# Block 1's attention rewritten: reversed queries, cumulative sums in two fp32r rounds, paired scores, first operands in halves

## The chip, the cores and the metric

One core of a Trainium2 chip runs the whole program in one launch. The metric is the device time of an execution in microseconds. A core has TensorE for matrix products, VectorE, ScalarE and GpSimd for the rest, SyncE for issuing loads, and 16 DMA engines that all queues share. Each engine works through its own list of instructions in order and waits at semaphores for others.

## The reference

Two transformer blocks over 256 tokens of width 1024, in fp32. Block 1: an RMS norm modulated by six vectors from `silu(c) @ w_ada`, one product with `w_in` for queries, keys and values of two attentions and two gates, and then the two attentions of 8 heads of 64. After them come gates, an output product, and a mixture of 64 experts. Block 2 is another norm, convolution, latent attention, a cross-attention to a memory `mem_2` (whose keys and values come from `w_mem_kv`), and 16 experts.

The change is in block 1's attentions and the opening. The first attention is stick-breaking, in blocks of 128 queries:

```
z = (q . k) * 0.125
log_rest = where(past, log_sigmoid(-z), 0)
log_skip = reversed cumulative sum of log_rest - log_rest
a = where(past, exp(log_sigmoid(z) + log_skip), 0);  o = a @ v
```

The second, of 256 tokens and so of a single block, is a softmax with a bias by distance:

```
s = (q . k) * 0.125 + rel_bias[head, t5_bucket(q_pos - k_pos)], -1e30 where k_pos > q_pos
o = softmax(s) @ v
```

## The kernel before

Activations lie with features on the partitions: x is `[128, 8, 256]`, eight chunks of 128 features by 256 tokens. Weights come in chunks of 1 MB (`[128, 2048]` fp32) through a ring of large tiles (`ring_tile`, `load`, L94 to L102), all issued by SyncE (`nc.sync`) in program order. A chunk is split in two halves into a high fp32r part (a cast on ScalarE, L210) and a low one (a subtraction on VectorE, L211), and every product is three rounds: high by high, high by low, low by high (`passes`, L217). A product whose operands are plain fp32 appears as two instructions in the trace, an fp32r one as one.

The opening: SyncE loads `vec`, `hm` (the memory, 1 MB), the first chunk of `w_mem_kv`, `x`, then pairs of `w_ada` chunks with the other `w_mem_kv` chunks between them. ScalarE's queue loads four small tables: `t5`, `w_router`, the router's bias row and `caprow`. `memk(i)` multiplies the memory by a chunk of `w_mem_kv` (48 products of 256 columns); it is called for 0, 1, 2, and after the loop for 2 and 3. `ada` (L304) multiplies a `w_ada` chunk by `silu(c)`, laid out with zeros in `scz`. When four pairs are done, `ada_cols` turns them into columns, and A1, `xr`, `h_hi` and `h_lo` follow (L383 to L388): h is the operand of all `w_in` products.

The bias of the second attention is a `[8, 384]` row table by distance, `rel`, made by one product of `t5` (L351) and stored to DRAM (L369). It is read back with overlapping rows as `relU` (row p begins p elements later) and turned upside down by four products with `flip`, a matrix with ones on the other diagonal (L379), copied by VectorE (L381).

`qkv` runs the chunks of one attention: `qk_chunk` (48 products a chunk, evacuated by ScalarE at L415) and `v_chunk`, with more `ada` between. In the first attention `scores` (L471) makes two groups of 64-row products, one for the heads on the lower 64 partitions and one for those on the upper, each in its own PSUM bank; the pool `s` has three banks. `softplus` computes log(1+exp(z)) with three ScalarE steps, one VectorE step and a mask on GpSimd; products with `ntri` (a triangle of -1) and `nones` (all -1) add the cumulative sum to the scores in PSUM (L518, L524, L525); `stick` takes the exponential and masks; `av` multiplies by the values. Block 128..255 goes first (`z1`), then the first 128 keys in two halves of heads (`z0`). The second attention (`mb_p`) adds the bias, does a softmax over the free axis, transposes the probabilities with `ident` (L559, L560, L567) and calls `av`.

The order on each engine is made when the program is built, from its dependencies and modelled times: later `w_in` chunks stand between the steps of an attention. `order(late, early)` fixes the order of two instructions by hand, `tc.issue_after` issues what is in its body behind a given instruction. Tiles made by `big(slot, ...)` share a slot; a new tile in it waits until the old one is read.

After block 1 the router's choice sets the order in which the experts' weights are loaded, and the expert loops follow.

## Time and profile before

| | us |
|---|---|
| median of 3 runs | 1609.36 (1609.12 to 1611.26) |
| profiled execution | 1608.48 |
| its span, first to last instruction | 1606.6 |
| TensorE busy | 1403.8 |
| VectorE busy | 595.0 |
| ScalarE busy | 415.0 |
| DMA | 524.78 MB, mean 327 GB/s |

The profile shows one execution. Busy times are unions of an engine's instructions; TensorE's instructions overlap, so the pace of products is read from their starts and not from their durations. "Idle before" is the time for which an engine stood before an instruction, with the one that ended it. The chain of waits begins at 801.22 us.

### The profile page before, as it was taken

How to read it: one execution, taken by the hardware profiler on the slowest of the kernel's cores; microseconds unless marked ns; L12 is line 12 of the kernel's file. 1: busy time of each engine (PE TensorE's matmuls, PEld its weight loads, DVE VectorE, ACT ScalarE, POOL GpSimd, SP SyncE). 2: the span in 40 equal slices, each digit the busy share in tenths (PEclk: the TensorE clock that was granted, in tenths of full speed). 3: DMA queues.
4: the chain of work that ended last, by engine and by line, in shares of the span. 5: the costliest groups of instructions: out<-in, count | busy, mean ns of one | idle time of the engine just before them, and what ended most of it. 6: DMA issues, size and time to landing. Idle time of an engine off the chain costs nothing.

```text
span 1606.6 us, 24192 instructions
## 1 busy us (share of the span) xinstructions
PE 1403.8 (87%) x9933; PEld 886.7 (55%) x9933; DVE 595.0 (37%) x1093; ACT 415.0 (26%) x741; POOL 98.7 (6%) x157
## 2 busy tenths in 40 slices
PE   6999999898999989999899999999796776676674
PEld 4787899653554435455498899998441221121221
DVE  6433655522222223343565666674330110110122
ACT  4453444321111112122255344453200000000001
POOL 1000101200000000000011110111100000000001
PEclk9999999999999999999999999999897787778776
DMA  8885755389999999999943345656499999999995
GB/s 326 345 344 207 292 192 199 109 357 419 419 419 420 419 420 419 421 420 420 410 171 134 129 171 192 217 217 254 182 420 421 422 420 420 421 422 420 420 421 215
DMA packets 74162, 524.78 MB, mean 327 GB/s; under 512 B 8282, under 2 KB 9890, under 8 KB 10562
## 3 DMA queue, kind: packets, MB, share of 16 engines
q1 hardware_dynamic: 72848, 519.35, 80.5%
q10 hardware_dynamic: 1202, 3.87, 0.6%
q8 instruction: 79, 1.29, 0.3%
q14 instruction: 33, 0.27, 0.0%
HBM read 521.01 MB, written 2.17 MB: 326 GB/s over the span
## 4 chain that ended last, share of the span: by engine, by line
DMA 25%; PE 21%; DVE 2%; issue 2%; ACT 1%; POOL 0%; DVEq 0%; SPq 0%; ACTq 0%; POOLq 0%
DMA w<-in_w_gu 15%; PE ps_d L217 13%; DMA w<-in_w_down 10%; PE ps_u L1613 1%; PE ps_s L217 1%; PE ps_s L1392 1%; PE ps_s L1391 1%; PE ps_t L1399 0%; ACT whl L210 0%; PE ps_t L1382 0%; PE ps_y L1682 0%; PE ps_s L1516 0%; PE ps_c L1604 0%; POOL tsm L1374 0%; DVE whl L211 0%
## 5 line engine op out<-in xcount | busy, mean ns | idle before, releaser
L211 DVE TENSOR_TENSOR whl<-w,whl 128x1024 fp32r<-128x1024 f32 x156 | 193.8, 1246 | 146.9 <-ACT whl L210 146.5
L950 PE MATMUL ps_u<-w,xg 128*32 128x512 f32 (+1 forms) x1152 | 213.1, 627 | 22.3 <-DMA w<-in_w_gu 22.3
L217 PE MATMUL ps_d<-h_hi,whl 128*128 128x256 f32 x1216 | 225.5, 284 | 1.1 <-ACT whl L210 1.1
L210 ACT CAST whl<-w 128x1024 fp32r<-128x1024 f32 x156 | 162.7, 1048 | 169.9 <-PE ps_d L217 149.5
L217 PEld LDWEIGHTS ps_d<-h_hi,whl 128*128 128x128 f32 x1216 | 189.2, 189 | 6.8 <-ACT whl L210 2.8
L217 PE MATMUL ps_d<-h_lo,whl 128*128 128x256 f32 x608 | 171.7, 282 | 0.0
L950 PEld LDWEIGHTS ps_u<-w,xg 128*32 128x32 f32 (+1 forms) x1152 | 62.9, 126 | 167.3 <-issue 122.8
L1613 PE MATMUL ps_u<-w,xgb 128*32 128x512 f32 x512 | 96.5, 832 | 50.8 <-DMA w<-in_w_gu 50.8
L217 PEld LDWEIGHTS ps_d<-h_lo,whl 128*128 128x128 f32 x608 | 114.3, 188 | 1.5 <-issue 1.3
L1613 PE MATMUL ps_u<-w,xga 128*32 128x512 f32 x512 | 94.4, 697 | 21.1 <-DMA w<-in_w_gu 21.1
L1682 PE MATMUL ps_y<-w,aT 128*32 128x256 f32 x1024 | 84.6, 473 | 27.0 <-DMA w<-in_w_down 22.9
L973 PE MATMUL ps_y<-w,aT 128*32 128x512 f32 (+1 forms) x576 | 95.9, 597 | 0.7 <-DMA w<-in_w_down_e 0.7
L956 DVE SCALAR_TENSOR_TENSOR act<-ps_u,wsl,sl 128x256 f32<-128x256 f32 x26 | 12.6, 484 | 200.5 <-ACT sl L954 200.5
L1670 DVE SCALAR_TENSOR_TENSOR act<-ps_u,wsl,sl 128x256 f32<-128x256 f32 x16 | 7.7, 484 | 212.6 <-ACT sl L1660 212.6
L1613 PEld LDWEIGHTS ps_u<-w,xgb 128*32 128x32 f32 x512 | 12.6, 125 | 124.7 <-DMA w<-in_w_gu 119.2
L1660 ACT ACTIVATE sl<-ps_u 128x256 f32<-128x256 f32 x16 | 6.1, 383 | 276.0 <-PE ps_u L1613 276.0
L991 DVE TENSOR_TENSOR y<-ps_c,y 128x512 f32<-128x512 f32 x92 | 63.0, 686 | 32.3 <-PE ps_c L982 32.3
L1682 PEld LDWEIGHTS ps_y<-w,aT 128*32 128x32 f32 x1024 | 33.9, 131 | 73.7 <-DMA w<-in_w_down 42.6
L954 ACT ACTIVATE sl<-ps_u 128x256 f32<-128x256 f32 x26 | 10.0, 384 | 215.6 <-PE ps_u L950 215.6
L981 PE MATMUL ps_c<-S,yy 128*128 128x256 f32 x208 | 62.7, 325 | 1.1 <-ACT whl L210 0.6
L211 DVE TENSOR_TENSOR yy<-ps_y,yy 128x512 fp32r<-128x512 f32 x52 | 36.0, 692 | 51.6 <-ACT yy L210 51.6
L884 PE MATMUL ps_g<-G,ht_hi 128*128 128x256 f32 x208 | 51.9, 283 | 3.2 <-DVE G L865 2.9
(492 smaller groups left out, 2227.5 us busy)
## 6 DMA issues: line engine op xcount, KB each, us to landing
w<-in_w_gu SPq DMA_DIRECT2D x256, 1024.0 KB, 19.8
w<-in_w_down_e SPq DMA_DIRECT2D x64, 1024.0 KB, 19.8
w<-in_w_down SPq DMA_DIRECT2D x64, 1024.0 KB, 19.8
w<-in_w_in SPq DMA_DIRECT2D x42, 1024.0 KB, 6.2
w<-in_w_ada SPq DMA_DIRECT2D x24, 1024.0 KB, 9.7
w<-in_w_mem_kv SPq DMA_DIRECT2D x4, 1024.0 KB, 14.1
w<-in_w_out SPq DMA_DIRECT2D x4, 1024.0 KB, 7.7
w<-in_w_conv_out SPq DMA_DIRECT2D x4, 1024.0 KB, 4.8
```

Of the source, the lines that this page charges most:

```text
L210: nc.scalar.copy(hi, src)
L211: eng.tensor_sub(lo, src, hi.bitcast(F32))
L217: nc.tensor.matmul(region, l, r, start=(start and u == 0), stop=(stop and u == 2), skip_group_check=True)
L884: nc.tensor.matmul(ps[:, a, :ng], ht_hi[:, b, k * P:(k + 1) * P], m, start=(b == 0), stop=False)
L950: nc.tensor.matmul(pg[o:o + w], xg[:, 4 * half + k, o:o + w], ws[j][:, k], start=(half == 0 and k == 0), stop=(half == 1 and k == 3), tile ...
L973: nc.tensor.matmul(py[o:o + w], self.aT[:, f, o:o + w], wd[j][:, f, h * 512:(h + 1) * 512], start=(f == 0), stop=(f == 1), tile_position=( ...
L981: nc.tensor.matmul(ps[:, a], self.yy[:, 0, k * P:(k + 1) * P], self.S, start=True, stop=False)
L991: nc.vector.tensor_add(y1[:, 2 * q:2 * q + 2], ps, y1[:, 2 * q:2 * q + 2])
L1391: nc.tensor.matmul(ps[:, b], qnT[:, h, b * P:(b + 1) * P], knT[:, h], start=True, stop=False)
L1392: nc.tensor.matmul(ps[:, b], qrT[r, h // 2, b * P:(b + 1) * P], krT[r, 0], start=False, stop=True)
L1613: mm = nc.tensor.matmul(pg[32 * j:32 * j + 32], xg[k][:, 32 * e:32 * e + 32], w[:, 512 * j:512 * j + 512], start=(k == 0), stop=(k == KD - ...
L1682: nc.tensor.matmul(py[32 * j:32 * j + 32, :256], aT[:, f, 32 * v:32 * v + 32], w[:, f, 256 * j:256 * j + 256], start=(v == 0 and f == 0), ...
```

## The change

`hm` and the first `w_mem_kv` chunk are each loaded by two DMAs of half the size, and that chunk's two halves are split ahead of the squares of `hm`. Three fp32 products of `ones` with `scz` (504 columns), whose result nobody reads, stand ahead of the first real products. The four small tables on ScalarE's queue are issued behind the last `hm_hi` instruction. `rel` is stored two rounds later; `relU` and the four flip products with their copies are gone. The bias is read straight into its tile, behind the first `qkv`, with its rows upside down; to match, the queries of the second attention are written in reversed order inside each block of 128 (a negative step on L415's output), and the transposes of the probabilities use `flip` in place of `ident`, which turns them back. In `softplus` the result is split into a high and a low fp32r part, and `ntri` and `nones` are fp32r, with two products each. All products of a `scores` call are ordered one behind another, lower and upper 64 rows in turn.

```diff
@@ -318,21 +318,31 @@
...
     hm = big(2, [P, KD, T], F32, "hm")
-    nc.sync.dma_start(hm, I["memT"])
+    for u in range(2):
+        nc.sync.dma_start(hm[:, 4 * u:4 * u + 4], I["memT"][:, 4 * u:4 * u + 4])
     hm_hi, hm_lo = big(4, [P, KD, T], F32R, "hm_hi"), big(11, [P, KD, T], F32R, "hm_lo")
-    wk = [load(I["w_mem_kv"][0])]
+    wk = [ring_tile()]
+    for u in range(2):
+        o = slice(1024 * u, 1024 * u + 1024)
+        nc.sync.dma_start(wk[0][:, o], I["w_mem_kv"][0][:, o])
     nc.sync.dma_start(xT, I["xT"])
...
                 lambda j, ps: nc.vector.tensor_mul(mem_k[:, 2 * i:2 * i + 2], ps,
-                                                   rm[:, None, :].to_broadcast([P, 2, T])), loaded=wk[i])
-
+                                                   rm[:, None, :].to_broadcast([P, 2, T])), loaded=wk[i],
+                parts=wk0 if i == 0 else None)
+
+
+    ps = bank("t")
+    for _ in range(3):
+        nc.tensor.matmul(ps[:, :504], ones, scz.rearrange("p k n -> p (k n)"), start=True, stop=True)
     gm = col("norm_memkv_g", KD)
     for k in range(KD):
-        nc.scalar.activation(hm_hi[:, k], hm[:, k], AF.Copy, scale=gm[:, k:k + 1])
+        hm_last = nc.scalar.activation(hm_hi[:, k], hm[:, k], AF.Copy, scale=gm[:, k:k + 1])
         nc.vector.scalar_tensor_tensor(hm_lo[:, k], hm[:, k], gm[:, k:k + 1], hm_hi.bitcast(F32)[:, k],
                                        op0=ALU.mult, op1=ALU.subtract)
+    wk0 = SP.chunk(wk[0], KD, 256)
     acc = pa.tile([P, T], F32, name="acc", tag="acc", bufs=2)
@@ -346,13 +356,13 @@
...
     t5 = big(9, [32, 776], F32, "t5")
-    nc.scalar.dma_start(t5, I["t5"])
+    with tc.issue_after(hm_last.ins):
+        nc.scalar.dma_start(t5, I["t5"])
     ps_r = bank("t")
...
     rel_d = dram.tile([8, 384], F32, name="rel_d")
-    relU = big(3, [P, 8, 256], F32, "relU")
     memk(0)
@@ -365,20 +375,11 @@
...
                 memk(i + 1)
-        if i == 0:
+        if i == 2:
             nc.sync.dma_start(rel_d, rel)
-        if i == 2:
-            nc.sync.dma_start(relU, bass.AP(tensor=rel_d.tensor, offset=rel_d.offset,
-                                            ap=[[1, P], [384, 8], [1, 256]]))
     ada_cols(ps_a, 0, 4)
...
     memk(3)
-    bias = big(11, [P, 8, 256], F32, "bias")
-    for i in range(4):
-        ps = bank("t")
-        f = nc.tensor.matmul(ps, flip, relU[:, 2 * i:2 * i + 2].rearrange("p a n -> p (a n)"), start=True, stop=True)
-        order(f, mm)
-        nc.vector.tensor_copy(bias[:, 2 * i:2 * i + 2].rearrange("p a n -> p (a n)"), ps)
     A1 = pa.tile([P, KD], F32, name="A1")
@@ -396,11 +397,12 @@
...
     wr = pa.tile([P, KD, 64], F32, name="wr")
-    nc.scalar.dma_start(wr, I["w_router"])
     rbias = const.tile([P, 64], F32, name="rbias")
-    nc.scalar.dma_start(rbias, I["router_bias"].to_broadcast([P, 64]))
     caprow = const.tile([1, 64], F32, name="caprow")
-    nc.scalar.dma_start(caprow, I["caprow"])
+    with tc.issue_after(hm_last.ins):
+        nc.scalar.dma_start(wr, I["w_router"])
+        nc.scalar.dma_start(rbias, I["router_bias"].to_broadcast([P, 64]))
+        nc.scalar.dma_start(caprow, I["caprow"])
@@ -412,7 +414,11 @@
...
         def evac(j, ps):
-            nc.scalar.activation(qk[nm][:, 2 * c:2 * c + 2], ps, AF.Copy, scale=0.125 if nm[0] == "q" else 1.0)
+            o = qk[nm][:, 2 * c:2 * c + 2]
+            if nm == "q_mb":
+                o = bass.AP(tensor=o.tensor, offset=o.offset + P - 1, ap=[o.ap[0], [P, 4], [-1, P]])
+                ps = ps.rearrange("p a (b t) -> p (a b) t", b=2)
+            nc.scalar.activation(o, ps, AF.Copy, scale=0.125 if nm[0] == "q" else 1.0)
         SP.feat(I["w_in"][base + c], h_hi, h_lo, 256, KD, evac)
@@ -450,39 +456,43 @@
...
-    ntri = pa.tile([P, P], F32, name="ntri")
-    nc.gpsimd.memset(ntri, -1.0)
-    nc.gpsimd.affine_select(out=ntri, in_=ntri, pattern=[[-1, P]], base=0, channel_multiplier=1,
+    nones = pa.tile([P, P], F32R, name="nones")
+    nc.vector.tensor_scalar(nones, ones, -1.0, 0.0, op0=ALU.mult, op1=ALU.add)
+    ntri = pa.tile([P, P], F32R, name="ntri")
+    nc.gpsimd.affine_select(out=ntri, in_=nones.bitcast(F32), pattern=[[-1, P]], base=0, channel_multiplier=1,
                             compare_op=ALU.is_ge, fill=0.0)
-    nones = pa.tile([P, P], F32, name="nones")
-    nc.vector.memset(nones, -1.0)
-    o_hi = big(5, [P, 8, T], F32R, "o_hi")
-    o_lo = big(6, [P, 8, T], F32R, "o_lo")
-    spl, aTs, keep = quarters(12, "spl"), quarters(13, "aTs"), None
-
-    oc = {"sb": (o_hi[:, :4], o_lo[:, :4]), "mb": (o_hi[:, 4:], o_lo[:, 4:])}
+    aTs, keep = quarters(13, "aTs"), None
...
         pss = [bank("s").rearrange("p (h q) -> p h q", q=nr) for _ in range(2)]
+        mms = []
         for i in range(n):
...
                 q = slice(64 * r, 64 * r + 64)
-                nc.tensor.matmul(pss[r][:, i], lhs[q, i0 + i, l0:l0 + nl], rhs[q, i0 + i, r0:r0 + nr],
-                                 start=(i == 0), stop=(stop and i == n - 1))
+                mms.append(nc.tensor.matmul(pss[r][:, i], lhs[q, i0 + i, l0:l0 + nl], rhs[q, i0 + i, r0:r0 + nr],
+                                            start=(i == 0), stop=(stop and i == n - 1)))
+                if len(mms) > 1:
+                    order(mms[-1], mms[-2])
         return pss
-    def softplus(ps, nq, name):
+    sp_hi, sp_lo = big(12, [P, 4, 512], F32R, "sp_hi"), big(7, [P, 4, 512], F32R, "sp_lo")
+
+    def softplus(ps, nq, q):
+
         t = pa.tile([P, 512], F32, name="sp_t", tag="t512", bufs=3)
...
         nc.scalar.activation(t, t, AF.Ln, bias=1.0)
-        sp = (keep() if nq == P else spl()).rearrange("p (h q) -> p h q", q=nq)
-        nc.vector.scalar_tensor_tensor(sp.rearrange("p h q -> p (h q)"), f, 0.0, t, op0=ALU.max, op1=ALU.add)
-        nc.gpsimd.affine_select(out=sp, in_=sp, pattern=[[0, 512 // nq], [1, nq]], base=0, channel_multiplier=-1,
+        nc.vector.scalar_tensor_tensor(t, f, 0.0, t, op0=ALU.max, op1=ALU.add)
+        t = t.rearrange("p (h q) -> p h q", q=nq)
+        nc.gpsimd.affine_select(out=t, in_=t, pattern=[[0, 512 // nq], [1, nq]], base=0, channel_multiplier=-1,
                                 compare_op=ALU.is_gt, fill=0.0)
-        return sp
+        hi = sp_hi[:, q].rearrange("p (h q) -> p h q", q=nq)
+        lo = sp_lo[:, q].rearrange("p (h q) -> p h q", q=nq)
+        split(t, hi, lo)
+        return hi, lo
@@ -509,21 +519,29 @@
...
     qkv("sb", v_sb, 0)
+    bias = big(11, [P, 8, 256], F32, "bias")
+    nc.sync.dma_start(bias, bass.AP(tensor=rel_d.tensor, offset=rel_d.offset, ap=[[1, P], [384, 8], [1, 256]]))
+    o_hi = big(5, [P, 8, T], F32R, "o_hi")
+    o_lo = big(6, [P, 8, T], F32R, "o_lo")
+    oc = {"sb": (o_hi[:, :4], o_lo[:, :4]), "mb": (o_hi[:, 4:], o_lo[:, 4:])}
     mem_kd = dram.tile([P, KD, T], F32, name="mem_kd")
...
     z1 = scores(qk["k_sb"], qk["q_sb"], 4, 0, P, P, P, P)
-    s1 = [softplus(z1[r], P, "sp1") for r in range(2)]
+    s1 = [softplus(z1[r], P, r) for r in range(2)]
     for r in range(2):
-        nc.tensor.matmul(flat(z1[r]), ntri, flat(s1[r]), start=False, stop=True, skip_group_check=True)
+        for u in range(2):
+            nc.tensor.matmul(flat(z1[r]), ntri, flat(s1[r][u]), start=False, stop=(u == 1), skip_group_check=True)
     a1 = [stick(z1[r], P) for r in range(2)]
...
         z0 = scores(qk["k_sb"], qk["q_sb"], 2, 2 * j, 0, P, 0, T)
-        s0 = [softplus(z0[r], T, "sp0") for r in range(2)]
+        s0 = [softplus(z0[r], T, 2 + r) for r in range(2)]
         for r in range(2):
-            nc.tensor.matmul(flat(z0[r]), ntri, flat(s0[r]), start=False, stop=False, skip_group_check=True)
-            nc.tensor.matmul(z0[r][:, :, P:], nones, s1[r][:, 2 * j:2 * j + 2], start=False, stop=True,
-                             skip_group_check=True)
+            for u in range(2):
+                nc.tensor.matmul(flat(z0[r]), ntri, flat(s0[r][u]), start=False, stop=False, skip_group_check=True)
+            for u in range(2):
+                nc.tensor.matmul(z0[r][:, :, P:], nones, s1[r][u][:, 2 * j:2 * j + 2], start=False, stop=(u == 1),
+                                 skip_group_check=True)
         a0 = [stick(z0[r], T) for r in range(2)]
@@ -548,6 +566,7 @@
...
+    spl = quarters(12, "spl")
     qkv("mb", v_mb, 6)
@@ -556,15 +575,15 @@
...
             for i in range(2):
-                nc.tensor.transpose(ps[:, i, :P], p0[r][:, 2 * j + i], ident)
-                nc.tensor.transpose(ps[:, i, P:], p1[r][:, i, :P], ident)
+                nc.tensor.transpose(ps[:, i, :P], p0[r][:, 2 * j + i], flip)
+                nc.tensor.transpose(ps[:, i, P:], p1[r][:, i, :P], flip)
             a = aTs().rearrange("p (h q) -> p h q", h=2)
...
             for i in range(2):
-                nc.tensor.transpose(ps[:, 2 * r + i], p1[r][:, i, P:], ident)
+                nc.tensor.transpose(ps[:, 2 * r + i], p1[r][:, i, P:], flip)
         a1 = aTs().rearrange("p (h q) -> p h q", h=4)
...
         av("mb", v_mb, j, a0, [a1[:, 2 * r:2 * r + 2] for r in range(2)])
```

## Rows read from the trace of the kernel before

**Rows 1.** The page's first part: busy us (share of the span) and instructions.

```profile
PE 1403.8 (87%) x9933; PEld 886.7 (55%) x9933; DVE 595.0 (37%) x1093; ACT 415.0 (26%) x741; POOL 98.7 (6%) x157
```

**Rows 2.** Busy time by stage: length, busy (instructions), granted clock, DMA share, GB/s.

```profile
15.08:65.24 50.16, 48.15 (x340) 36.92 (x341) 29.24 (x58) 19.93 (x40) 0.74 (x2) 1.00 0.92 372
...
107.75:131.00 23.25, 23.00 (x136) 15.56 (x133) 9.53 (x11) 16.20 (x29) 7.31 (x12) 1.00 0.64 258
131.00:167.50 36.50, 36.50 (x307) 30.20 (x307) 13.15 (x12) 14.99 (x18) 0.00 (x0) 1.00 0.77 282
167.50:191.50 24.00, 22.44 (x173) 17.79 (x170) 18.53 (x36) 11.54 (x38) 6.53 (x16) 1.00 0.59 220
...
282.00:310.00 28.00, 21.90 (x124) 18.51 (x121) 17.42 (x88) 13.13 (x28) 11.38 (x17) 0.88 0.37 137
...
350.00:800.00 450.00, 423.53 (x2670) 213.56 (x2662) 142.22 (x313) 77.21 (x148) 0.00 (x0) 0.97 1.01 420
```

**Rows 3.** Timeline of the opening: start, us, engine, line, names, count [idle before].

```profile
4.13 0.17 DVE L298 COPY scz<-sc 128x8 f32<-128x8 f32 x1 [2.24 <-ACT sc L295]
...
7.03 3.30 ACT L333 ACTIVATE hm_hi<-hm,c_vec 128x256 fp32r<-128x256 f32 x8 [2.93 <-DMA hm<-in_memT]
...
14.09 1.05 ACT L210 CAST whl<-w 128x1024 fp32r<-128x1024 f32 x1
...
16.21 2.51 DVE L211 TENSOR_TENSOR whl<-w,whl 128x1024 fp32r<-128x1024 f32 x2
...
28.50 0.39 PE L217 MATMUL ps_d<-hm_hi,whl 128*128 128x256 f32 x1
```

**Rows 4.** Busy time in stretches of 2 us of the opening, as in rows 2.

```profile
18.00:20.00 2.00, 2.00 (x11) 2.00 (x10) 1.93 (x7) 2.00 (x7) 0.00 (x0) 1.00 1.02 430
...
22.00:24.00 2.00, 2.00 (x14) 1.35 (x14) 1.61 (x4) 0.58 (x2) 0.00 (x0) 1.00 0.00 0
24.00:26.00 2.00, 2.00 (x20) 2.00 (x19) 0.00 (x0) 0.63 (x1) 0.00 (x0) 1.00 0.61 125
```

**Rows 5.** SyncE's waits from 0 to 60 us: total, times, longest.

```profile
SPq L369 <- DVE acc L150: 16.1, 1, 16.1
```

**Rows 6.** DMA issues at 7.1, at 37.7 and at the end: KB each, us to landing.

```profile
w<-in_w_mem_kv SPq DMA_DIRECT2D x1, 1024.0 KB, 14.1
...
w<-in_w_ada SPq DMA_DIRECT2D x1, 1024.0 KB, 13.0
...
out<-of SPq DMA_DIRECT2D x4, 256.0 KB, 2.6
```

**Rows 7.** Timeline around the first w_in product, columns as in rows 3.

```profile
54.30 1.07 PE L304 MATMUL ps_a<-w,scz 128*32 128x512 f32 x8
...
59.25 3.92 PE L379 MATMUL ps_t<-relU,flip 128*128 128x512 f32 x8
63.11 1.04 PE L304 MATMUL ps_a<-w,scz 128*32 128x512 f32 x2
...
64.15 2.94 ACT L210 CAST whl<-w 128x1024 fp32r<-128x1024 f32 x3
...
65.24 0.39 PE L217 MATMUL ps_d<-h_hi,whl 128*128 128x256 f32 x1 [1.08 <-ACT whl L210]
```

**Rows 8.** Attention products: groups by form (busy us, mean ns | idle), then single lines.

```profile
L524 PE MATMUL ps_s<-spl,ntri 128*128 128x512 f32 x8 | 4.4, 631 | 0.0
L471 PE MATMUL ps_s<-qk_sb 64*128 64x256 f32 x16 | 4.2, 396 | 0.0
...
L471 PE MATMUL ps_s<-qk_sb 64*128 64x128 f32 x16 | 1.2, 285 | 0.0
...
L471 PE MATMUL ps_s<-qk_mb 64*128 64x256 f32 x16 | 3.8, 396 | 0.0
...
L471 PE MATMUL ps_s<-qk_sb x4: 376/377/378, 108.7 to 109.4; 64*128 64x256 f32 x4
...
L471 PE MATMUL ps_s<-qk_sb x2: 376/428/480, 115.0 to 115.3; 64*128 64x256 f32 x2
```

## The prediction

> **What bounds the kernel now.** I read the page's head first: TensorE is busy 87% of the span [rows 1]. The chain of waits reaches back only to the second half of the run and says nothing of the part that changes. So busy time by stage comes next [rows 2]. TensorE is busy 48.2 of 50.2 us in the opening, 23.0 of 23.25 in the first attention, 36.5 of 36.5 in the second set of projections and 22.4 of 24.0 in the second attention. Block 1 up to its routing is thus bound by TensorE's own instructions, apart from the first 15 us, in which it has none. From 282 to 310 us (routing) the DMA share is 0.37, and from 350 to 800 us it is 1.01 at 420 GB/s. The expert weights' stream is the bound there and does not push from behind: a microsecond cut from block 1 should move the routing, the stream and all that follows by a microsecond. Last I read the timeline of the opening and the groups by form of the two attentions.
>
> **The opening.** The first products wait in turn for three things. hm lands at 7.03 us; ScalarE then makes hm_hi until 10.3, squares and loads a table, so that the first half of the first weights is cast only at 14.09 and its low part begins on VectorE at 16.21 [rows 3]. TensorE is then slow: 11 products start in 18 to 20 us, 20 in 24 to 26 [rows 4]. Both rows print a granted clock of 1.00, but about 0.213 us a start is the pace of 256 columns at the 1.2 GHz level, and the 0.117 of later that of the 2.4 GHz one; the engine had been idle for 15 us. Meanwhile SyncE stands 16.1 us before it stores rel, and every load behind it on that queue stands too [rows 5]; the DMA share is 0.00 in 22 to 24 us [rows 4].
>
> After the change hm lands without 0.39 MB of small tables beside it, about 1 us earlier (0.39 MB at 420 GB/s), and its first half some 1.2 us before that. hm_hi then ends near 8.1 us, two casts of 1.05 near 10.2, the first low part (1.25) near 10.4: the first products start at about 10.5. The idle products can start when scz is written, at 4.3 us [rows 3]. They are six instructions of 0.85 us (twice the 0.43 derived below, at the lower level), so they end near 9.5 and delay nothing. The first 48 products then end near 16.2 us. I cost the four table issues on ScalarE's queue at nothing: ahead of the casts they would delay a first round that has until 20 us.
>
> For that gain is not kept whole. The second weights of this kind were issued at 7.02 us and took 14.1, landing at 21.1 [rows 6], behind the same 7 MB as after the change. I take 20 us, between 18.4 (all at full rate) and 21.1. Cast and low part add some 2, so the second round starts at about 21.8 instead of 28.50 [rows 3]: 6.7 us won. The first ada and the statistics, some 4 us of products, fit into the gap.
>
> From 28.5 to 59.25 us TensorE has 30.75 us of products almost without a wait. Then come 3.92 us of bias products, an ada load's 1.04 and 1.08 idle, while h is made; from the last ada product of this stretch (54.30 plus 1.07) to the first w_in product (65.24) it is 9.9 us, ended by ScalarE [rows 7]. Removing the bias products, and four VectorE copies beside them, shortens that chain by nothing: they are its cover. They pay only if the last ada products move ahead of other work. These can: their load, issued at 37.7 us, took 13.0 and landed at 50.7 [rows 6]. Without the stall and without relU's 1 MB, eight 1 MB loads at 2.5 us follow the one that I put at 20 us: it lands at 40. What TensorE then has left is 21.8+30.75+2.1 (two ada loads) = 54.6 us, 10.6 less than 65.24. If it keeps its order, the gain stays 6.7. I take 9.5, nearer to the end that the loads allow.
>
> relU's transfer now fetches bias behind the first qkv's loads; the DMA share is 0.77 in the next projections [rows 2], which hide it, and its reader is 60 us away. Uncovered it costs 2.5 us. The store of rel, two rounds later, is behind some 8 MB already issued, 20 us of transfers; a stall like the old one of 16.1 fits into that: 0.
>
> **Attention.** One fp32 round becomes two fp32r rounds. Four fp32 instructions of 256 columns start within 0.65 us, 0.216 apart, so 512 columns take 0.43 [rows 8]. ntri has 12 of 512 (8 of them in the row; two instructions for each of six products), nones 8 of 256 by its four calls: 5.2+1.7 = 6.9 us. In fp32r a 256-column start takes 0.117, so the same count costs 12*0.234+8*0.117 = 3.7, and 3.2 us are won. Scores: the 128-column ones already run in pairs, 16 in 1.2 us; the 256-column ones do not, 16 in 4.2 and 16 in 3.8 us [rows 8]. Fully paired they would take 2.4 each: 3.2 us. But a group needs two of three banks, and its first product may still go alone as soon as one is free, three steps for four: 1.6. I take 2.4, between them.
>
> The splits add six ScalarE copies, half of the 1.05 us cast each, 3.2 us in all, and six VectorE subtractions, and each softplus is later by about 1.3 us. ScalarE is busy 16.2 of 23.25 us there [rows 2], 19.4 after it. A late product on TensorE holds up what stands behind it, the casts likewise behind the copies; 12 half-chunks of the next weights (2.8 us of products for each cast) are there to fill. I charge 1.5 us of new idle, between 0 and the 5.6 won. The reversed write of the queries is not in the trace: two copies on a ScalarE with 21.5 of 36.5 us free [rows 2], 0 if as fast as now, 3.2 us if four times slower (half a cast, twice), and hidden; I take 0. Flip for ident in the transposes leaves count and shape: 0. keep no longer holds the softplus, so this no longer waits for mem_k's store: 0.
>
> **Sum.** 9.5+3.2+2.4-1.5 = 13.6 us. The profiled execution took 1608.48 us, 1.9 more than its span, and is 0.88 under the median of the runs shown: 1608.5-13.6+0.9 = 1595.8 us.
>
> **Rivals.**
> (a) The split softplus makes ScalarE the bound: the 5.6 us of the first attention and the scores come back as waits. For it: ScalarE's 16.2 us. Against: the filler. 1608.5-9.5+0.9 = 1599.9 us.
> (b) TensorE keeps its order around the last ada and stands idle where the bias products were: 2.8 us less, 1598.6.
> (c) The halves load worse than whole tiles. A 256 KB store lands 2.6 us after its issue [rows 6], 0.6 of it data; if 2 us were added for each of two extra pieces, all loads come 4 us later: 1599.8. Against: the loads behind one another come at 430 GB/s [rows 4], so a fixed part is hidden in the queue. The Trainium skill's page DMA: Bandwidth & Descriptors, section Bandwidth, speaks against this edit: pieces of at least 1 MiB keep three quarters of the peak. No run here shows a load of half that size.
> (d) The idle products end too long before the real ones, and the engine is slow again: 48 products at 0.213 us end at 20.7, an ada round of 1.9 at 22.6, and the second round starts 0.8 us later: 1596.6. The Trainium skill's page TensorE: Matmul & The Clock Gate, section Why this matters for your kernels, warns that idle gaps between bursts take the rate back. The slow products after 15 us of idling [rows 4] agree with it.
> (e) Slower: the fixed order makes the first half of a 256-column group wait for the second's bank. In the old trace one half went at 108.7 us and the other at 115.0 [rows 8]. Four groups held back 6.3 us each cost 25 us with nothing to fill them, 1621; under 14 of filler in these 25 the gain is gone. Against: the filler of 131 to 167.5 us is 36.5 us long [rows 2].
> (f) No change: waits in the routing take the gain back, 1609.
>
> **Numbers.** Forecast 0.53, (a) 0.12, (b) 0.12, (c) 0.06, (d) 0.07, (e) 0.05, (f) 0.05. The forecast's own range is 1591 to 1600: its best end is 10.6 with the second weights at 18.4 (1.6 more) and 6.4 in the attentions, 1590.8. The 1.6 us that TensorE idles in the second attention may go too: 1589. (a) and (b) or (c) together reach 1604. Range 1588 to 1604, without (e) and (f). 0.2%, 3.2 us, is about what a measurement tells from no change: faster 0.88, same 0.06, slower 0.06.
>
> **What will show it.** The first real product near 10.5 us, 0.117 us from start to start; the second round near 21.8; no DMA share under a half from 12 to 40 us; the first w_in product near 55.7 (58.5 by b). In the attention, fp32r products of 512 columns 0.23 us apart, 256-column scores in pairs, under 2 us idle on TensorE. The routing as long as before, 13 to 14 us earlier. I am wrong if the first w_in product comes under 5 us earlier, if the attentions add over 6 us of idle, or if the full stream that runs from 350 us starts no earlier.

## The result and the profile after

The changed kernel takes 1618.35 us, median of five runs (1617.38 to 1619.07), against 1610.2 of the kernel before: ratio 1.0051, 95% interval 1.0039 to 1.0062. It is 0.5% slower. The forecast was 1595.8, at most 1604.

TensorE has as much to do as before [rows 1]. Engines of the changed kernel: busy us (share), instructions.

```profile
PE 1404.5 (87%) x9931; PEld 890.1 (55%) x9931; DVE 599.0 (37%) x1095; ACT 418.3 (26%) x747; POOL 100.7 (6%) x156
```

The changed kernel by stage, in the order of [rows 2]: opening, first attention, second projections, second attention, routing, stream.

```profile
12.67:70.69 58.02, 50.77 (x333) 39.34 (x333) 30.57 (x61) 23.56 (x48) 6.65 (x8) 0.85 0.82 331
114.85:143.30 28.45, 24.09 (x155) 18.73 (x152) 15.60 (x18) 22.22 (x36) 6.72 (x10) 0.88 0.61 245
143.30:179.60 36.30, 36.06 (x288) 27.76 (x286) 12.45 (x12) 13.73 (x18) 1.75 (x2) 1.00 0.75 281
179.60:203.60 24.00, 21.79 (x173) 17.03 (x170) 18.70 (x36) 11.42 (x38) 6.53 (x16) 1.00 0.60 228
294.00:322.00 28.00, 22.05 (x123) 18.66 (x122) 17.35 (x88) 13.16 (x28) 11.36 (x17) 0.88 0.36 133
360.00:810.00 450.00, 422.39 (x2686) 213.78 (x2678) 141.22 (x310) 77.76 (x149) 0.00 (x0) 0.98 1.01 418
```

Two stages are longer, the opening (58.0 us for 50.2) and the first attention (28.5 for 23.3). In both TensorE now idles, 7.3 and 4.4 us (2.0 and 0.3 before), and the mean granted clock printed fell from 1.00 to 0.85 and 0.88. The opening's 1.00 before is too high: it also stands over the slow products up to 22 us, 22 starts in 18 to 22 us where 0.117 us a start gives 34. Starts of the same instructions in the two traces say where the 10.7 us between the spans come from:

```
first instruction of      before    after   shift
first memory chunk         15.95    12.67    -3.3
second memory chunk        28.50    29.73    +1.2
third memory chunk         36.62    44.65    +8.0
w_in products              65.24    70.69    +5.5
first softplus            108.94   116.06    +7.1
gates after attention     224.48   236.61   +12.1
end of span              1606.55  1617.28   +10.7
```

**The opening.** Timeline of the changed kernel, columns as in [rows 3].

```profile
3.80 5.41 PE L339 MATMUL ps_t<-scz,ones 128*128 128x504 f32 x6 [3.80 <-DVE scz L298]
...
9.98 1.71 ACT L342 ACTIVATE hm_hi<-hm,c_vec 128x256 fp32r<-128x256 f32 x4 [2.47 <-DMA hm<-in_memT]
...
20.80 0.50 PE L157 MATMUL ps_t<-ones,acc 128*128 128x1 f32 x4
...
21.52 0.20 ACT L170 ACTIVATE rs<-ms 128x2 f32<-128x2 f32 x1 [3.90 <-DVE ms L165]
...
28.18 0.20 ACT L170 ACTIVATE rs<-ms 128x2 f32<-128x2 f32 x1 [3.91 <-DVE ms L165]
...
28.52 1.98 ACT L210 CAST whl<-w 128x1024 fp32r<-128x1024 f32 x2
...
30.47 2.77 DVE L370 TENSOR_TENSOR xr<-xT,rrow 128x256 f32<-128x256 f32 x8
...
33.16 2.35 DVE L211 TENSOR_TENSOR whl<-w,whl 128x1024 fp32r<-128x1024 f32 x2
...
34.43 0.79 PE L217 MATMUL ps_d<-hm_hi,whl 128*128 128x256 f32 x2 [2.51 <-DVE whl L211]
```

Granted clock and DMA in the changed kernel's opening: length, PE busy (instructions), clock, DMA share, GB/s.

```profile
14.00:18.00 4.00, 4.00 (x19) 0.50 1.01 425
...
30.00:34.00 4.00, 1.92 (x8) 0.54 1.00 400
34.00:38.00 4.00, 3.57 (x16) 0.50 1.02 372
38.00:42.00 4.00, 4.00 (x25) 0.68 1.00 420
...
72.00:76.00 4.00, 4.00 (x25) 0.66 0.47 158
```

The second memory weight landed at 23.12, but its cast was issued at 28.52. Ahead of it in ScalarE's list stands x's statistic (28.18). That waits for x's squares, and these stand behind the memory's statistic (21.52), whose sums TensorE does only at 20.80, after 36 products of the first chunk. On VectorE the eight multiplications that make xr (2.77 us) stand ahead of the low half of the same weight. So TensorE gets two products of the second chunk, the six of a modulation load (`ada`), and idles 2.51 us; until about 41 us it then runs at the lower level, 1.2 GHz, where the kernel before was at 1.00 and full pace from 26 on. Before, the weight landed at 21.09 and the cast was issued at 21.11, in front of x's statistic:

```profile
21.11 1.04 ACT L210 CAST whl<-w 128x1024 fp32r<-128x1024 f32 x1 [1.01 <-DMA w<-in_w_mem_kv]
...
27.20 0.20 ACT L170 ACTIVATE rs<-ms 128x2 f32<-128x2 f32 x1 [2.58 <-DVE ms L165]
```

The planner, which orders each engine's instructions when the program is built, had made other lists; the diff has no line on that order. The Trainium skill's page TensorE: Matmul & The Clock Gate (section Architectural detail: the array is 16× 32×32, not 1× 128×128) calls the queues of ScalarE and VectorE strictly first in, first out; the trace agrees: ScalarE stands idle for 3.91 us ahead of x's statistic at 28.18 while the landed weight waits behind it, 5.4 us in all.

After 14 to 20 and 34 to 41 us, a third slow stretch follows the wait ahead of the first w_in product, which is 2.34 us now: 72 to 76 us show 0.66. In the kernel before, after 1.08 us:

```profile
72.00:76.00 4.00, 4.00 (x37) 1.00 0.73 254
```

From the first w_in product to the first softplus it is 45.4 us instead of 43.7; that is the step from +5.5 to +7.1 in the table.

**The first attention.** Timeline of the changed kernel.

```profile
114.86 1.59 PE L473 MATMUL ps_s<-qk_sb 64*128 64x128 f32 x18
...
116.06 1.08 ACT L485 ACTIVATE sp_t<-ps_s 128x512 f32<-128x512 f32 x2 [2.35 <-PE ps_s L473]
...
119.11 1.04 ACT L210 CAST whl<-w 128x1024 fp32r<-128x1024 f32 x1
...
120.20 0.58 PE L217 MATMUL ps_d<-h_hi,whl 128*128 128x256 f32 x1 [3.74 <-ACT whl L210]
```

No weight of the second projections is cast ahead of the softplus, so TensorE has nothing to do for 3.74 us. Before, two half-chunks were:

```profile
106.48 1.99 ACT L210 CAST whl<-w 128x1024 fp32r<-128x1024 f32 x2
108.94 1.08 ACT L478 ACTIVATE sp_t<-ps_s 128x512 f32<-128x512 f32 x2 [0.46 <-PE ps_s L471]
```

The load of bias and the store of mem_k are issued at 99.0 and 99.5 ahead of those weights, which land at 113.8 and 116.3; before, at 104.2 and 106.7. The landing alone does not explain the wait: ScalarE is idle for 2.35 us ahead of the softplus at 116.06 and the first weight is there at 113.8, but the cast stands behind the softplus in its list.

Groups of the changed kernel that answer to [rows 8]:

```profile
L473 PE MATMUL ps_s<-qk_sb 64*128 64x256 f32 x16 | 4.6, 457 | 0.1
L473 PE MATMUL ps_s<-qk_mb 64*128 64x256 f32 x16 | 3.0, 409 | 0.1
...
L541 PE MATMUL ps_s<-sp_hi,ntri 128*128 128x512 f32 x4 | 1.8, 462 | 0.0
L541 PE MATMUL ps_s<-sp_lo,ntri 128*128 128x512 f32 x4 | 1.7, 424 | 0.1
L534 PE MATMUL ps_s<-sp_hi,ntri 128*128 128x512 f32 x2 | 1.4, 710 | 0.0
```

### The profile page after: what moved, and what is told of

Same layout as the page of the kernel before. It is cut to its first block, busy times and chain, and to the rows that moved or that the text cites. A ratio compares the mean times of both kernels' runs of the same rounds, so it can differ in the third digit from the quotient of the medians.

```text
span 1617.3 us, 24194 instructions
## 1 busy us (share of the span) xinstructions
PE 1404.5 (87%) x9931; PEld 890.1 (55%) x9931; DVE 599.0 (37%) x1095; ACT 418.3 (26%) x747; POOL 100.7 (6%) x156
## 4 chain that ended last, share of the span: by engine, by line
DMA 25%; PE 20%; DVE 2%; issue 2%; ACT 1%; POOL 0%; DVEq 0%; SPq 0%; ACTq 0%; POOLq 0%
DMA w<-in_w_gu 15%; PE ps_d L217 13%; DMA w<-in_w_down 10%; PE ps_s L217 1%; PE ps_u L1632 1%; PE ps_s L1411 1%; PE ps_s L1410 1%; PE ps_t L1418 0%; PE ps_t L1401 0%; ACT whl L210 0%; PE ps_y L1701 0%; PE ps_s L1535 0%; POOL tsm L1393 0%; DVE whl L211 0%; PE ps_c L1623 0%
## 5 line engine op out<-in xcount | busy, mean ns | idle before, releaser
L1701 PE MATMUL ps_y<-w,aT 128*32 128x256 f32 x1024 | 80.4, 455 | 30.2 <-DMA w<-in_w_down 26.4
L1010 DVE TENSOR_TENSOR y<-ps_c,y 128x512 f32<-128x512 f32 x92 | 62.9, 685 | 32.3 <-PE ps_c L1001 32.3
## 6 DMA issues: line engine op xcount, KB each, us to landing
w<-in_w_ada SPq DMA_DIRECT2D x24, 1024.0 KB, 10.5
w<-in_w_out SPq DMA_DIRECT2D x4, 1024.0 KB, 10.3
```

The costliest lines, as they stand in the source:

```text
L1010: nc.vector.tensor_add(y1[:, 2 * q:2 * q + 2], ps, y1[:, 2 * q:2 * q + 2])
L1701: nc.tensor.matmul(py[32 * j:32 * j + 32, :256], aT[:, f, 32 * v:32 * v + 32], w[:, f, 256 * j:256 * j + 256], start=(v == 0 and f == 0), ...
```

## The experiments

Ratios are to the kernel before on the same chip; 0.001 is 1.6 us. Differences between kernels below are taken from these ratios. A trace shows one execution, which need not be a typical one: that of the late bias below took 1609.34 us against a median of 1612.26, that of the control 1609.20 against 1604.42. The changed kernel and the one with the late bias have the same list on every engine up to 66 us, and yet the first softplus starts at 116.1 in one trace and at 112.6 in the other. So a trace tells mechanisms and the ratios tell times.

**Which half loses.** *Opening undone:*

```
-    for u in range(2): hm and wk[0] in halves
+    hm, wk[0] whole
-    three products of ones and scz; wk0 = SP.chunk(wk[0], KD, 256)
-    with tc.issue_after(hm_last.ins): t5, w_router, router_bias, caprow
+    the same four where they stood; rel_d stored at i == 0
```

> The changed kernel with its opening undone: memory and first weight loaded whole, no idle products, first weight cast where it was, small tables issued first on ScalarE's queue, rel written at the first modulation pair. The attention change is kept whole. Theory A (two separate losses): the opening lost 7.1 us up to the first softplus and the first attention 5.0, so this one is 7 us under the changed kernel and still 0 to 3 us over the kernel before (about 1611); the first softplus starts at about 109 to 111, and the first attention is still about 5 us longer. Theory B (one loss: the late opening alone makes the first attention late too, by what the queues then hold): both losses go, and the attention's own gain of about 2 us shows: 1606 to 1609, with first w_in weights for the second half there before the softplus. Theory C (the split of the softplus costs ScalarE): as A, but with TensorE waiting for the casts of sp_hi all through the first attention, not once.

1606.33, ratio 0.9985 (0.9976 to 0.9994): 10.6 us under the changed kernel. The attention half is not a loss by itself. The first w_in load lands at 49.8 instead of 53.2 and the first w_in product starts at 62.38 instead of 65.24: relU's megabyte no longer stands ahead of it. A and C fall, B holds.

*Opening alone*, on the kernel before:

```
+    halves, three idle products, wk0, issue_after as in the diff; relU, bias products and attention as before
```

> The kernel before with the edits of the opening alone: loads in halves, six idle products, first weight cast ahead of the squares, small tables issued after the memory's eight scalings. Relative bias by its four products and its load as before, attention as before. Theory A: 5 to 7 us slower than the kernel before (1615 to 1617), the second memory chunk's first product at about 34 instead of 28.5. Rival (the missing bias products, not the loads, are what the opening lost: they were cover before the first w_in product): within 2 us of the kernel before, and the first w_in product at about 65 to 67.

1616.14, ratio 1.0035 (1.0024 to 1.0046). The second chunk starts at 27.8 (29.7 in the changed kernel), but TensorE idles three times ahead of it and in it (1.31, 0.69, 1.43 us) and runs at 0.50 until 38; the third chunk starts at 42.5 instead of 36.6. The opening loses without any change in the attention.

*The load of bias:*

```
-    nc.sync.dma_start(bias, ...)      # behind qkv("sb")
+    nc.sync.dma_start(bias, ...)      # behind qkv("mb")
```

> The changed kernel with one line moved: the load of the relative bias (1 KB pieces) is issued behind the second half's w_in loads instead of ahead of them. Theory E (the bias load holds up those weights on the sync queue, no weight is cast ahead of the softplus, and TensorE idles 3.7 us and then runs slow): w_in for the second half lands by 107, two casts stand ahead of the first softplus, the idle stretch after the first scores shrinks to under 1.5 us, and the first attention is 4 to 6 us shorter: 1612 to 1614. Rival C (the softplus split on ScalarE is the loss): the stretch from the first softplus to the end of the first attention stays within 1 us of the changed kernel's, and so does the time.

1612.26, ratio 1.0018 (1.0009 to 1.0027), 5.3 us under the changed kernel. The run's timeline:

```profile
110.14 1.99 ACT L210 CAST whl<-w 128x1024 fp32r<-128x1024 f32 x2
111.22 2.36 DVE L211 TENSOR_TENSOR whl<-w,whl 128x1024 fp32r<-128x1024 f32 x2 [9.83 <-ACT whl L210]
111.40 1.59 PE L473 MATMUL ps_s<-qk_sb 64*128 64x128 f32 x18
112.59 1.09 ACT L485 ACTIVATE sp_t<-ps_s 128x512 f32<-128x512 f32 x2 [0.46 <-PE ps_s L473]
```

The weights land from 107.9 on, two casts stand ahead of the softplus, the idle stretch is gone, and from the first softplus to the gates it is 113.3 us instead of 120.6 (115.5 before). E holds.

Its opening is the changed kernel's, instruction by instruction, but the memory is complete at 8.98 us instead of 9.95 and the slow products end sooner. The sums for the memory's statistic and all that hangs on them come 2.2 us earlier:

```profile
14.00:18.00 4.00, 4.00 (x27) 0.71 1.03 391
```

```profile
18.59 0.50 PE L157 MATMUL ps_t<-ones,acc 128*128 128x1 f32 x4
...
32.22 0.50 PE L217 MATMUL ps_d<-hm_hi,whl 128*128 128x256 f32 x2 [3.23 <-DVE whl L211]
```

*Both repairs*, opening undone and bias late:

> The attention change alone with the opening of before, and the relative bias loaded behind the second half's w_in loads: the two repairs together. If the two losses add (opening undone: 3.1 us under the kernel before; bias load moved: 6.1 us under the changed kernel, of which some 4 us are its place), it comes out at 1600 to 1604, faster than the kernel before by 5 to 9 us. Rival (with the old opening two casts already stood ahead of the softplus, so the place of the bias load is worth nothing more): within 1.5 us of the run with the opening undone, about 1606.

1607.04, ratio 0.9975 (0.9965 to 0.9985). The rival won: with the old opening at least one cast stands ahead of the softplus in either case (one, three), and the place of the load is worth nothing clear of the noise. Its price shows only with the new opening.

**Which edit of the opening.** Each was put back alone on the two repairs; two more runs undid one in a kernel with the new opening. *Halves:*

```
+    for u in range(2): hm[:, 4u:4u+4]; wk[0][:, 1024u:1024u+1024]
```

> The kernel of the two repairs with one edit of the opening put back: memory and first weight loaded in halves. Theory L (halves are loaded more slowly than whole tiles and delay all that stands behind them): 2 to 4 us over the kernel of the two repairs, the second half of the memory landing after 9 us and the second chunk's weight 1.5 to 2 us later. Theory D (order alone loses): within 1 us.

0.9981 (0.9972 to 0.9990): nothing that the time shows. The trace does show what theory L expects of the loads. The second half of the memory with halves, then the whole memory in the kernel of the two repairs:

```profile
9.52 1.70 ACT L338 ACTIVATE hm_hi<-hm,c_vec 128x256 fp32r<-128x256 f32 x4 [0.76 <-DMA hm<-in_memT]
```

```profile
6.92 3.30 ACT L334 ACTIVATE hm_hi<-hm,c_vec 128x256 fp32r<-128x256 f32 x8 [2.94 <-DMA hm<-in_memT]
```

The second chunk's weight lands at 22.4 instead of 21.0. In nine kernels with halves the memory is complete at 8.1 to 10.3 us, in eleven without at 6.6 to 8.2. The Trainium skill's page DMA: Bandwidth & Descriptors, section Bandwidth, asks for pieces of at least 1 MiB; these landings agree, but with the old opening they cost no time clear of the noise.

*Early cast:*

```
+    wk0 = SP.chunk(wk[0], KD, 256)     # ahead of squares(pa, acc, hm, ...)
```

> The kernel of the two repairs with one edit of the opening put back: the first weight is cast ahead of the squares and their statistic. Theory D (order): 3 to 6 us over the kernel of the two repairs, the first product earlier but the second chunk's first product after 32 us. Theory L (the loads lose): within 1 us or faster.

1603.87, 0.9967 (0.9955 to 0.9979): no loss. Here five of x's eight squares stand before the memory's statistic. The second weight's cast waits for x's statistic here too (landed at 21.2, cast at 25.3), but the first low half stands ahead of xr's multiplications; TensorE idles 1.57 us and stays at 1.00.

*Idle products:*

```
+    for _ in range(3): nc.tensor.matmul(ps[:, :504], ones, scz...)
```

> The kernel of the two repairs with one edit of the opening put back: six idle products ahead of the first real ones. Theory I0 (they end by about 9 us, several us before the first real product, and change nothing): within 0.8 us of the kernel of the two repairs, and the first memory products start 0.213 us apart as without them. Rival (they help the clock): granted clock 1.00 at once and 2 us faster. Rival (they push TensorE's own first work, the sums of the squares, back): slower by over 1 us.

0.9974 (0.9963 to 0.9985): nothing, I0 holds.

*Late tables:*

```
+    with tc.issue_after(hm_last.ins): t5, w_router, router_bias, caprow
```

> The kernel of the two repairs with one edit of the opening put back: the small tables issued after the memory's eight scalings. Here the first weight's cast and x's squares stand behind the memory's statistic in both, so ScalarE's order hardly differs. Theory O (order, through the early cast): within 1.5 us of the kernel of the two repairs, 1606 to 1608.5. Theory Q (the late tables themselves: their landing holds loads on the sync queue back): 3 to 6 us slower, 1610 to 1613, with loads on that queue issued in the moment a table lands.

0.9976 (0.9967 to 0.9985): nothing.

*Early cast undone* in the changed kernel:

```
-    wk0 = SP.chunk(wk[0], KD, 256)
```

> The changed kernel with the first weight's cast put back where it stood, after the squares and their statistic; halves, idle products and late tables kept. Theory D (order on ScalarE and TensorE: the early cast lets 36 products go ahead of the statistic, so the memory's statistic, x's squares, x's statistic and the second chunk's cast are all late and TensorE stands idle 2.5 us before it): the second chunk starts at about 28 to 30 instead of 34.4, and the run is 3 to 6 us under the changed kernel (1612 to 1615), though the first product starts later than 12.7. Rival (the loads are what is late: halves and the late tables): the second chunk still starts after 33, within 2 us of the changed kernel.

1616.12, 1.0040 (1.0026 to 1.0054), 1.8 us under the changed kernel, with intervals that overlap; the second chunk starts at 32.3 and runs without a wait, where the changed kernel's went on at 34.4. Between the two.

*Tables early again* in the one with the late bias:

```
-    with tc.issue_after(hm_last.ins):  (both)
```

> The changed kernel with the relative bias loaded late (as in the run that moved that one line, 1612) and the small tables issued first on ScalarE's queue again; halves, idle products and the early cast of the first weight stay. Theory O (order: with the late tables the list that ScalarE follows has x's squares behind the memory's statistic, which itself waits for sums that TensorE does after 36 products; each of the other three edits alone costs nothing): with the tables early x's squares stand ahead of that statistic, the second chunk starts before 31 us instead of 34, and the run is 5 to 9 us under the one with the late bias: 1603 to 1607. Rival (halves, idle products and early cast cost together what none costs alone): 1610 to 1613.

1610.87, 1.0009 (1.0000 to 1.0018): the rival's number, theory O falls. Two of x's eight squares stand ahead now and the second chunk starts at 26.25, but xr's multiplications still stand ahead of its low half, TensorE idles 3.24 us and runs at 0.50 from 31 on. So none of these four edits loses alone; they lose together. The later store of rel was not tried alone.

**The order itself.** x's work written after the second chunk and held there:

```
+    cast1, sub1 = halves_of            # the second chunk's last cast and low half
+    r1 = rstd_of(pa, xT, KD, D, late=cast1)          # order(ln, cast1)
+    order(nc.vector.tensor_mul(xr[:, k], xT[:, k], r1), sub1)
```

In the changed kernel:

> The changed kernel, all its edits, with one thing fixed by hand: x's statistic (its first function on ScalarE) comes behind the casts of the second memory chunk's weight, and its eight multiplications on VectorE behind that chunk's low half. Theory W (that order is the opening's loss: it makes TensorE stand idle some 3 to 4 us ahead of the second chunk, and after it the clock is at its lower level for 7 us): the second chunk starts before 28 us, no stretch at 0.50 after it, the first w_in product by 64 instead of 70.7, and the run 5 to 8 us under the changed kernel: 1609 to 1613. Rival (the loads or the idle products lose, the order only follows them): within 2 us of the changed kernel.

1607.57, 0.9992 (0.9983 to 1.0001): 9.5 us under the changed kernel, more than W asks. The second chunk starts at 27.2 as W says, but 30 to 34 us show 0.69 and the first w_in product comes at 67.1, not by 64. And with the bias late:

> The same order by hand, with the relative bias loaded late as well (1612.3 without the order). Theory W: 1604 to 1607, as fast as the kernels with the old opening or faster. If only the late bias matters: 1611 to 1613.

1602.18, 0.9958 (0.9945 to 0.9971). Then the control, in which the same lines are only written further down:

```
-    r1 = rstd_of(pa, xT, KD, D); xr = ...       # behind memk(0)
+    the same lines, not ordered                   # behind memk(1)
```

> A control: the changed kernel with the late bias (1612.3, ratio 1.0018) in which x's statistic and its multiplications are only written further down in the program, without the fixed order; the lists of the engines keep x's work ahead of the second memory chunk. Theory W (the order is what the hand-ordered run of 1602 gained): within 2 us of the late-bias run, ratio 1.000 to 1.003, TensorE idle 3 us ahead of the second chunk and at 0.50 after it. Rival (writing it elsewhere moves tiles, and loads behind the attention then run at 424 instead of 420 GB/s): ratio 0.996 to 0.999, the stretch behind the attention 5 us shorter.

1604.42, 0.9969 (0.9958 to 0.9980). The rival's number. Timeline of the control, then its clock in one stretch, then both of the kernel with the order held:

```profile
27.69 0.20 ACT L170 ACTIVATE rs<-ms 128x2 f32<-128x2 f32 x1 [3.90 <-DVE ms L165]
28.04 1.98 ACT L210 CAST whl<-w 128x1024 fp32r<-128x1024 f32 x2
...
32.26 0.80 PE L217 MATMUL ps_d<-hm_hi,whl 128*128 128x256 f32 x2 [2.55 <-DVE whl L211]
```

```profile
30.00:34.00 4.00, 1.74 (x8) 0.50 1.02 405
```

```profile
24.03 1.99 ACT L214 CAST whl<-w 128x1024 fp32r<-128x1024 f32 x2 [0.64 <-issue]
...
27.30 0.20 ACT L170 ACTIVATE rs<-ms 128x2 f32<-128x2 f32 x1 [1.27 <-DVE ms L165]
28.46 0.51 PE L220 MATMUL ps_d<-hm_hi,whl 128*128 128x256 f32 x2 [1.05 <-DVE whl L214]
```

```profile
30.00:34.00 4.00, 4.00 (x36) 1.00 1.01 405
```

The mechanism is as W says: with the order held the idle stretch is 1.05 us, the clock stays at 1.00, and the first softplus comes at 110.7 instead of 114.5. But most of the ratio came with the control (0.0049 under the late bias alone), whose trace has the idle stretch and the slow clock of the changed kernel. Behind the attention its stream runs faster. The last expert stage, length, PE, clock, DMA share, GB/s, in the kernel before and in the control:

```profile
1250.00:1400.00 150.00, 104.80 (x735) 0.77 1.01 421
```

```profile
1250.00:1400.00 150.00, 101.98 (x739) 0.79 1.01 424
```

All five kernels with x's lines moved have 424 there, all others 421; between this control, the kernel with the order held and the one with the late bias the lists of the engines behind the opening are the same. So W's two ratios cannot be taken as the price of the order. Like for like, held against the control, it is 1.8 us by the ratios, with intervals that overlap. The 3.8 us at the first softplus are no price either, since the execution that the control's trace shows lies 4.8 us over its median. That the order is the opening's whole loss is not shown.

**The attention's own terms**, on the two repairs. *One fp32 pass, no split:*

```
-    hi, lo = split softplus; ntri, nones in F32R, two products each
+    softplus, ntri, nones in F32, one product each
```

> The kernel of the two repairs (attention change alone, 1607.0 beside a before of 1609.8) with the cumulative sums in one pass of fp32 again: no split of the softplus, half the products. If the two passes are worth what the prediction put on them (3.2 gained, 1.5 of it given back by the splits): 1.5 to 2 us slower. If the splits cost what the passes gain: within 0.8 us. If the first attention is bound by ScalarE (each split adds a cast to it): 2 to 4 us faster.

0.9992 (0.9981 to 1.0002) against 0.9975: the two passes gain some 2.7 us net, splits paid, though the intervals overlap a little.

*No fixed order of the scores* (the `order(mms[-1], mms[-2])` left out):

> The kernel of the two repairs without the fixed order of the scores' products. If the pairing is worth what the prediction put on it (2.4 us, most of it where groups stand alone): 1 to 3 us slower. Rival (the program's own order pairs them in any case, or the groups stand beside a ScalarE that is the bound): within 0.8 us.

0.9964 (0.9952 to 0.9977) against 0.9975: the pairing gains nothing; it differs by 1.8 us the other way, and the intervals overlap.

**A faster version.** Two repairs, early cast, order held, no fixed score order, rel stored at i == 2, `memk(2)` once:

> What helped, together: old opening with the early cast of the first weight, x's statistic ordered behind the second chunk, rel written at the third modulation pair (so that the loads behind it on the sync queue aren't held), the third memory chunk computed once, scores without the fixed order, bias loaded late. If the opening is bound by the last modulation load, which then lands at about 44 to 46 instead of 51: first w_in product at 56 to 58 and 1597 to 1600. If the loads' landing isn't the bound: 1602 to 1605.

1602.89, 0.9953 (0.9940 to 0.9966): the second case. The last modulation weights have landed by about 42, yet TensorE does the fourth chunk first and later idles 6.2 us. With `order(first product of memk(3), last modulation product)` added:

> The kernel that puts together what helped (1602.9, ratio 0.9953), with one order more: the fourth memory chunk's products come behind the last modulation products on TensorE. In that kernel the last modulation weights have landed by about 42 and yet the modulation row is copied at 54, since TensorE does the fourth chunk first, and then stands idle 6.2 us ahead of the first w_in product. If the fourth chunk fills that idle stretch: modulation row at about 48, first w_in product at 57 to 59 instead of 64, and 1597 to 1599 (ratio 0.992 to 0.994). If the w_in weights or the casts that wait for the fourth chunk's buffers are late then: within 2 us of 1602.9.

1595.14, ratio 0.9908 (0.9891 to 0.9924): 0.9% faster than the kernel before, and a little more than was expected. Its timeline:

```profile
48.68 0.68 DVE L318 COPY ada_row<-ps_a 128x512 f32<-128x512 f32 x1
...
58.43 0.38 PE L222 MATMUL ps_d<-h_hi,whl 128*128 128x256 f32 x1 [2.08 <-ACT whl L214]
```

w_in's first product is 6.8 us earlier than before. The trace gains 13.0 us: 5.2 at the first softplus, 3.0 in the attentions, 4.8 behind them with the faster stream.
`memk(2)` once, alone beside the early cast, had been tried before:

> The kernel of the two repairs with the early cast of the first weight put back (the fastest so far, 1603.9), and the third memory chunk computed once instead of twice (48 products of 0.117 us fewer, 5.6 us of TensorE, and two casts). If TensorE bounds the stretch before the first w_in product: 1599 to 1601. If those products only fill time in which TensorE waits for the last modulation weights: within 1.5 us of 1603.9.

1605.30, 0.9981 (0.9972 to 0.9990): it only lengthened the idle stretch ahead of w_in, to 5.6 us.

## Why the prediction was wrong

The sum counted 9.5 us won in the opening and 4.1 in the attentions. In the two traces the first w_in product comes 5.5 us later, the stretch to the first softplus is 1.7 longer, the attentions 5.0 longer, and the rest 1.4 shorter: 10.7 lost.

- **"Cast and low part add some 2, so the second round starts at about 21.8"** is the step that failed. The weight landed at 23.1, outside the 18.4 to 21.1 allowed, and from there to the round's full run at 34.43 it was 11.3 us: the cast came 5.4 us later, and the low half ended behind xr's multiplications. The estimate took the list of the old trace as fixed and only moved its times; that each engine's order is itself made anew was weighed for TensorE alone. So 9.5 us won became 5.5 lost at the first w_in product. Shown: the place, the idle stretch, the slow clock, and that the idle stretch shrinks to 1.05 us with the order held. Not settled: which pair of edits tips the lists, and the order's price in time.
- **First products at 10.5**: 12.67, since the second half of hm landed at 9.95; whole it landed at 7.01. The halves do this by themselves: 9.5 with halves alone. The prediction had the memory about 1 us earlier than before, not 3 us later.
- **Rival (c)** was right in kind: in all kernels with halves the memory came some 1 to 3 us later than the 7.0 of the kernel before. Its price of 4 us did not show with halves alone (0.9981 against 0.9975).
- **Rival (d)** was right in kind and too cheap: idle products ended at 9.21, TensorE idled 3.46 us and 14 to 18 us show 0.50. Idle products alone cost nothing, but here the sums for the memory's statistic stand behind 36 of the slow products, and x's squares, the cast and the second round behind the sums. 34 of them at 0.117 us from 13.93 would have ended near 17.9 instead of 20.80: an estimate of 2.9 us, not 0.8. The late-bias kernel, with the same lists, had a shorter slow stretch and earlier loads, and its second round ran on 2.2 us earlier. The second slow stretch, from 34 us on, no rival named.
- **Last modulation load at 40**: it landed at 43.9 (50.7 before), and the DMA share is full from 10 to 58 us. Right in kind, but TensorE was no longer ready for it. The fastest version shows the gain that was there.
- **"Removing the bias products shortens that chain by nothing: they are its cover"**: as far as the traces tell, right; TensorE idles 2.34 us there instead of 1.08. With the opening undone the first w_in product came 2.9 us earlier and its load 3.4, with relU's megabyte and the products both gone; no run parts the two.
- **bias "behind the first qkv's loads ... hide it"**: wrong. Its reader is 60 us away; the price was at the weights queued behind it on SyncE and at their casts' place in ScalarE's list: 5.3 us in this opening, nothing clear of the noise in the old one.
- **Sums 3.2 won, 1.5 of idle lost**: about right net (1.7 said, 2.7 measured). **Scores 2.4 won**: mis-sized; mb's groups fell from 3.8 to 3.0 us, sb's rose from 4.2 to 4.6, and without the fixed order nothing is lost. With the old opening and the late bias the attentions are 1.3 to 2.6 us shorter, not 4.1.
- **Rival (b)** forecast 2.8 us lost at the place of the bias products. The idle stretch at w_in grew by 1.3, and the slow clock after it took 1.7 more; that the two come near 2.8 is luck. **(a) and (e)** did not happen. No routing or stream took time back: from the gates on the changed kernel is 1.4 us shorter.

## What to carry to other kernels

Where a planner makes the engines' lists, an edit that is free by itself can reorder work far from it: after any change to early loads or casts, compare each engine's order ahead of the first stall, and hold the few orders that matter by hand. When a load is put on a queue, price what stands behind it there, not only its own reader. An idle stretch on TensorE can be paid twice, once more when the clock falls after it. And moving lines for an experiment can change something else: here a control showed that most of the gain came from that.

## What the runs showed of the hardware

Idle stretches of 2.5 to 3.7 us were followed by several us at 0.50 (changed kernel at 34 and 120 us, control at 32, tables early again at 31); those of 1.05 to 1.57 were mostly not, though one run showed 0.69 in 30 to 34 us after 1.06. Between them it was either: in seven kernels with the old opening, or one edit of it, TensorE idled 1.80 us ahead of w_in, between the same products; four of the traces then show 0.50, and from the first w_in product to the first softplus it is 45.6 us, three show 1.00, and it is 43.7 to 44.1. Six idle products that ended 3.46 us ahead of the real ones did not keep the clock.

The printed clock can miss the first slow stretch: in 18 to 22 us the kernel before starts 22 products and the one with idle products alone 20, and the profile prints 1.00 for the first and 0.50 for the second.

Loads at a full DMA share came at 424 instead of 421 GB/s in all five kernels in which x's tiles are taken later, two of them with the same lists behind the opening as a kernel at 421. In these five traces it is 1376.0 to 1379.5 us from the gates to the end, in the fifteen others 1379.7 to 1383.8; no run here shows why.
